# RWKV stage: TensorE in the order of emission, projection banks emptied one step later, weight transfers apart from their casts

## Chip, cores and metric

One core of a Trainium2 chip runs the whole program. The metric is the device time of one execution in microseconds (us); lower is better. TensorE is written PE, VectorE DVE, ScalarE ACT, GpSimd POOL, and the queue that issues most transfers SP.

## The reference

One decoder layer on x (1 x 1024 x 1024, float32): a shared RMSNorm, one input projection, two parallel branches of 16 heads (head size 64), an output projection, a residual and a final RMSNorm. The branch that matters here is the RWKV-7 recurrence:

```
p = rms_norm(x) @ w_in                    # 1024 x 8320
p_tm = p + (shift_by_one(p) - p) * mu     # r, k, v and two low-rank inputs
a = sigmoid(a0 + a_lo @ a_up);  decay = exp(-exp(-softplus(-(w0 + tanh(w_lo) @ w_up)) - 0.5))
state = state * w_t + (state @ -kk_t) (kk_t * a_t) + v_t k_t      # for each of 1024 tokens
y_t = state @ r_t
y = (group_norm(y) + bonus) * silu(gate)
```

The other branch is a dilated sliding-window attention over the same projection. Both go through w_out.

## The kernel before

The RWKV stage works in chunks of 64 tokens. A **unit** is one pair of heads on one half of the sequence (512 tokens, 8 chunks); there are 16 units, and two that follow each other (h = 0, here called even, and h = 1, odd) share a pair of heads. `rwkv` (L284) walks over p = -2 to 15. In each round unit p is in its recurrence (`chain`), unit p+1 in the inversion of its triangular matrices (`late`, `invert`), unit p+2 in its preparation (`prepare`, `products`), and unit p-1 is finished (`finish`). Each of these functions returns steps with the number of one of 24 slots (`NSLOT`); slot by slot the steps are called, and after the steps of a slot `advance(n)` emits n matmuls (4 in the rounds 0 to 12) of the input projection, which runs along through the whole stage as a stream (`stream`, L182).

The recurrence takes three slots per chunk, and each slot is one link of a chain that goes back and forth between three engines:

- slot 3c: `first` multiplies the state Sd into the banks z and T on PE; `spread` copies z to zd, one half on DVE (L704), the other on ACT (L705). [...]
- slot 3c+1: `second` multiplies zd on PE, and `spread` makes ud of it (L707 on DVE, L708 on ACT).
- slot 3c+2: `third` multiplies ud into T on PE, and `spread` makes the next Sd (L707, L708).

All of that is one form of PE matmul on the page (L693: z<-Sd, T<-Vd, T<-Sd, z<-zd, T<-ud, z<-Vd), and the three spreads are what PE waits for. The projection matmuls (L179, 128 x 512, 24 of them for a bank pq) depend on none of it.

Around these lie, in every unit: the products pa of `products` (L559, 16 matmuls on 64 of the rows of PE's array), the small products of the inversion xq, dq, x (L634 and L646 with 32 matmuls of 16 x 16, L663 and L674 with 16 of 32 x 32), transposes through PE, decay and bonus matmuls; on ACT the exponentials W and Ux (L428, L433) of the scans I that DVE makes (L422), the copies Vd (L513), a (L438), the copies Y of the recurrence's output (L745) and its squares ysq (L762); on DVE the inversion's columns TB, UB (L604, L606), the mean gs of Y (L756) and its subtraction (L758).

The projection itself asks two things of the other engines. `wload` (L161) fetches the 256 KB halves of a weight tile (wraw) and splits each into wh (cast on ACT, L170) and wl (subtraction on DVE, L171; on POOL for the attention columns); `stream` calls it for the next job ahead of the first matmul of the current one. `take` empties a full bank pq, for r, k and v by `shift` (ACT L213, then DVE L216).

Which instruction stands where on an engine is not decided by this text alone: a scheduler simulates the program and gives each engine, at each point of its simulated time, the ready instruction that was emitted first. The order that it writes is then fixed, and on the chip each engine executes its own in that order, waiting at its head where an input is late.

Of the kernel before, what the change touches and what calls it, by code (L numbers as in the profile page):

```python
# [33 lines left out]
WARM = (1, 0)  # L34
V_AT = (-2, 3, -1)
# [10 lines left out]
class Kern:  # L46
# [114 lines left out]
    def wload(self, src, wp, eng):  # L161

        nc = self.nc
        wl = wp.tile([128, KT, 128], F32R, name="wl")
        wh = wp.tile([128, KT, 128], F32R, name="wh")
        for i in range(2):
            raw = wp.tile([128, KT // 2, 128], F32, name="wraw")
            ks = slice(4 * i, 4 * i + 4)
            nc.sync.dma_start(out=raw, in_=src[i * 512:(i + 1) * 512].rearrange("(kt p) c -> p kt c", p=128))
            nc.scalar.copy(out=wh[:, ks], in_=raw)  # L170
            eng.tensor_tensor(out=wl[:, ks], in0=raw, in1=wh[:, ks].bitcast(F32), op=ALU.subtract)  # L171
        return wh, wl
# [9 lines left out]
    def stream(self, jobs):  # L182
# [3 lines left out]
        w = load(jobs[0])  # L186
        for i, (_, halves, take) in enumerate(jobs):
            wn = load(jobs[i + 1]) if i + 1 < len(jobs) else None
            for h in halves:
                q = self.ps_proj.tile([128, HALF], F32, name="pq", tag="proj")  # L190
                steps = self.proj_steps(w, h, q)
                for m in steps[:-1]:
                    m()
                    yield
                steps[-1]()
                take(h, q)
                yield
            w = wn
# [85 lines left out]
    def rwkv(self, pairs=range(NPAIR), apairs=range(NPAIR)):  # L284
        nc = self.nc
        with ExitStack() as ctx:
# [40 lines left out]
            N = len(units)  # L327
            self.flow = self.stream(self.jobs(units, apairs))
# [6 lines left out]
            self.lora_w(units[0])  # L335
            for p in range(-2, N):
# [3 lines left out]
                if dC:  # L340
                    put(enumerate(self.chain(dC, get(p + 1) if dC["h"] == 0 else None)))
# [8 lines left out]
                if get(p + 3) and get(p + 3)["h"] == 0:  # L350
                    ev[12].append(lambda d=get(p + 3): self.lora_w(d))
# [18 lines left out]
    def lora_w(self, d):  # L370
# [6 lines left out]
        hi = [self.mid.tile([128, 128], F32R, name=f"lhi{i}", bufs=1) for i in range(2)]  # L377
        lo = self.llo
        for i in range(2):
            a, b = slice(64 * i, 64 * i + 64), slice(64 - 64 * i, 128 - 64 * i)  # L380
            nc.scalar.copy(out=hi[i][a], in_=raw[a])
            nc.scalar.copy(out=hi[i][b], in_=raw[a])
            nc.gpsimd.tensor_tensor(out=lo[i][a], in0=raw[a], in1=hi[i][a].bitcast(F32), op=ALU.subtract)
        d["lw"] = hi, lo

    def prepare(self, d):
# [66 lines left out]
        def norm():  # L453
# [8 lines left out]
            V.reciprocal(out=rn, in_=rn)  # L462
            d["rn1"] = self.mid.tile([64, NC_], F32, name="rn1", bufs=3)
            S.copy(out=d["rn1"], in_=rn[64:128])
# [20 lines left out]
        def bonus_parts():  # L485
            rs = d["rs"]
            V.scalar_tensor_tensor(out=rs, in0=rs, scalar=self.hrk[:, pr:pr + 1], in1=d["ks"], op0=ALU.mult, op1=ALU.mult)
            bh, bl = d["bs"] = [self.tmp(t, n, dt=F32R) for t, n in (("kr3", "bh"), ("vr3", "bl"))]
# [101 lines left out]
    def invert(self, d, U):  # L590
# [86 lines left out]
        def m4c():  # L677
# [4 lines left out]
            (22, m4), (23, m4c)]  # L682
# [481 lines left out]
```

## Time and profile before

| | |
|---|---|
| median of 3 runs | 1554.56 us (1554.13 to 1555.15) |
| the profiled execution | 1555.3 us |
| its span in the profile | 1553.6 us |
| PE busy | 1486.1 us (96%) |
| DVE busy | 1009.3 us (65%) |
| ACT busy | 897.6 us (58%) |
| POOL busy | 442.0 us (28%) |
| granted PE clock, mean of the span | 0.998 |

The profiled execution took 1555.3 us, 1.7 us more than its span and 0.7 us more than the median. PE busy counts from the start of a matmul's record to its modelled end; records overlap, so a busy share near 100% does not say that PE takes a new matmul as often as it could.

### The profile page before, as it was taken

The page shows a single profiled execution, that of the slowest core. Times are in us where ns is not written, and L with a number is a line of the kernel's source. Part 1 is how long each engine was busy: PE and PEld are TensorE (multiplying, and loading weights), DVE is VectorE, ACT ScalarE, POOL GpSimd, SP SyncE. Part 2 cuts the span into 40 slices and gives each one's busy share as a digit, 9 for nine tenths or more (in the row PEclk, how much of TensorE's full clock was granted, in tenths as well). Part 3 has the DMA queues.
Part 4 walks back from the last instruction along what each step waited for, and adds up shares of the span by engine and source line. Part 5 has one row for each costly group of instructions (what it writes and reads, how often), then busy time and mean ns, then how long its engine had stood idle before and what let it go on. Part 6 is the DMA issues. An engine that isn't in the chain of part 4 may idle for free.

```text
span 1553.6 us, 29135 instructions
## 1 busy us (share of the span) xinstructions
PE 1486.1 (96%) x10721; PEld 1201.3 (77%) x10721; DVE 1009.3 (65%) x2776; ACT 897.6 (58%) x2080; POOL 442.0 (28%) x563
## 2 busy tenths in 40 slices
PE   5999999999999999999999999999999999899997
PEld 4877777777777777777777788888888888787886
DVE  6866776667776677766743557667676666956144
ACT  6655666666676666666643556555565565655221
POOL 3211111111111121112211534334443343456442
PEclk9999999999999999999999999999999999999999
DMA  6321111111111111111111201111111111426452
GB/s 199 90 48 33 41 40 39 41 34 40 47 32 41 47 33 41 39 38 41 34 39 34 70 28 42 35 35 34 38 52 34 36 55 55 159 92 203 142 161 99
DMA packets 178829, 94.87 MB, mean 61 GB/s; under 512 B 58413, under 2 KB 164606, under 8 KB 178686
## 3 DMA queue, kind: packets, MB, share of 16 engines
q1 hardware_dynamic: 174942, 86.19, 19.4%
q10 hardware_dynamic: 3744, 6.82, 1.3%
q8 instruction: 84, 1.38, 0.4%
q14 instruction: 59, 0.48, 0.1%
HBM read 75.01 MB, written 17.83 MB: 60 GB/s over the span
## 4 chain that ended last, share of the span: by engine, by line
PE 60%; DVE 17%; ACT 16%; issue 3%; DMA 2%; POOL 1%; SPq 0%; DVEq 0%; ACTq 0%; POOLq 0%
PE pq L179 28%; PE oq L1048 10%; PE o L994 3%; PE z L693 3%; PE T L693 3%; PE mp L921 2%; PE sp L954 2%; ACT Y L745 1%; DVE I L422 1%; ACT MV L569 1%; PE sp L974 1%; ACT Vd L513 1%; DVE TB L604 1%; ACT shtmp L213 1%; PE pa L559 1%
## 5 line engine op out<-in xcount | busy, mean ns | idle before, releaser
L179 PE MATMUL pq<-xh,wh 128*128 128x512 f32 x1040 | 429.1, 413 | 0.0
L179 PE MATMUL pq<-xl,wh 128*128 128x512 f32 x1040 | 412.3, 396 | 0.0
L179 PE MATMUL pq<-xh,wl 128*128 128x512 f32 x1040 | 303.3, 409 | 0.0
L179 PEld LDWEIGHTS pq<-xh,wh 128*128 128x128 f32 x1040 | 195.9, 188 | 32.6 <-ACT xh L157 0.3
L179 PEld LDWEIGHTS pq<-xl,wh 128*128 128x128 f32 x1040 | 196.4, 189 | 30.9 <-DVE xl L158 0.4
L179 PEld LDWEIGHTS pq<-xh,wl 128*128 128x128 f32 x1040 | 184.5, 189 | 31.9
L1048 PE MATMUL oq<-ow,qr 128*128 128x512 f32 x512 | 161.9, 394 | 1.2 <-ACT ow L1029 0.6
L982 POOL TENSOR_TENSOR pl<-p,ph 128x512 fp32r<-128x512 f32 (+2 forms) x96 | 102.3, 1072 | 202.2 <-ACT ph L981 182.4
L923 DVE CUSTOM_DVE_ANT_0 mp<-mp,maskq 128x512 f32<-128x512 f32 (+1 forms) x192 | 105.5, 570 | 68.4 <-PE mp L921 59.9
L977 ACT ACTIVATE p<-p 128x512 f32<-128x512 f32 (+2 forms) x144 | 64.6, 452 | 104.2 <-DVE p L976 103.3
L171 POOL TENSOR_TENSOR wl<-wraw,wh 128x512 fp32r<-128x512 f32 x64 | 85.5, 1354 | 110.4 <-PE pq L179 58.4
L1043 POOL TENSOR_TENSOR vr<-kr,qr 128x512 fp32r<-128x512 f32 (+2 forms) x68 | 90.8, 1340 | 80.5 <-ACT qr L1042 70.0
L1048 PEld LDWEIGHTS oq<-ow,qr 128*128 128x128 f32 x512 | 95.9, 188 | 22.8 <-ACT ow L1029 1.1
L1048 PE MATMUL oq<-ow,vr 128*128 128x512 f32 x256 | 101.2, 395 | 1.9 <-POOL vr L1043 1.9
L170 ACT CAST wh<-wraw 128x512 fp32r<-128x512 f32 x138 | 80.7, 616 | 28.6 <-PE pq L179 23.4
L1042 ACT CAST qr<-kr 128x512 fp32r<-128x512 f32 (+2 forms) x68 | 40.2, 594 | 93.5 <-PE oq L1048 52.0
L976 DVE TENSOR_TENSOR p<-sp,maskt 128x512 f32<-128x512 f32 (+2 forms) x144 | 65.2, 457 | 43.3 <-PE sp L974 41.9
L570 POOL TENSOR_SCALAR_AFFINE_SELECT MV<-MV 64x512 f32<-64x512 f32 x64 | 47.8, 747 | 125.2 <-ACT MV L569 114.2
L708 ACT ACTIVATE ud<-z,rn 64x64 f32<-64x64 f32 x128 | 39.3, 307 | 65.3 <-DVE ud L707 63.6
L707 DVE TENSOR_SCALAR ud<-z,rn 64x64 f32<-64x64 f32 x128 | 34.3, 268 | 58.1 <-PE z L693 57.9
L693 PEld LDWEIGHTS T<-ud,TU 128*128 128x128 f32 x256 | 42.5, 188 | 34.8 <-ACT ud L708 28.2
L708 ACT ACTIVATE Sd<-T,dec 64x64 f32<-64x64 f32 x120 | 36.9, 307 | 53.5 <-DVE Sd L707 52.0
(236 smaller groups left out, 3158.4 us busy)
## 6 DMA issues: line engine op xcount, KB each, us to landing
wraw<-in_w_in_dram SPq DMA_DIRECT2D x138, 256.0 KB
kr<-mixd SPq DMA_DIRECT2D x60, 256.0 KB
oraw<-in_w_out_dram SPq DMA_DIRECT2D x16, 512.0 KB
xt<-in_x_dram SPq DMA_DIRECT2D x8, 512.0 KB
ld<-TU SPq DMA_DIRECT2D x32, 128.0 KB
mixd<-zt SPq DMA_DIRECT2D x16, 256.0 KB
mixd<-gt SPq DMA_DIRECT2D x16, 256.0 KB
xr<-in_x_dram ACTq DMA_DIRECT2D x16, 256.0 KB
```

What stands on the lines that cost most here:

```text
L170: nc.scalar.copy(out=wh[:, ks], in_=raw)
L171: eng.tensor_tensor(out=wl[:, ks], in0=raw, in1=wh[:, ks].bitcast(F32), op=ALU.subtract)
L179: return [lambda i=i, a=a, b=b: self.nc.tensor.matmul(q, lhsT=a, rhs=b, start=(i == 0), stop=(i == len(ops) - 1)) for i, (a, b) in enumera ...
L570: G.affine_select(out=f, in_=f, pattern=[[0, 4], [-1, 2], [1, 64]], compare_op=ALU.is_ge, fill=0.0, base=0, channel_multiplier=-1)
L693: mm = lambda out, w, x, start, stop: nc.tensor.matmul(out, lhsT=w, rhs=f2(x), start=start, stop=stop, skip_group_check=True)
L708: S.activation(out=out[er[1], 1], in_=q[0:64, 64:128], func=AF.Copy, scale=scale[1])
L923: V.tensor_tensor_reduce(out=mp[:, :kn], in0=mp[:, :kn], in1=self.maskq[:, v0:v0 + kn], op0=ALU.add, op1=ALU.max, scale=1.0, scalar=-3e38, ...
L976: V.tensor_tensor(out=p[:, :qn], in0=sp[:, :qn], in1=self.maskt[:, u0:u0 + qn], op=ALU.add)
L977: S.activation(out=p[:, :qn], in_=p[:, :qn], func=AF.Exp)
L982: G.tensor_tensor(out=pl[:, :qn], in0=p[:, :qn], in1=ph[:, :qn].bitcast(F32), op=ALU.subtract)
L1043: nc.gpsimd.tensor_tensor(out=ml, in0=raw, in1=mh.bitcast(F32), op=ALU.subtract)
L1048: nc.tensor.matmul(q, lhsT=m[:, i], rhs=v, start=(k == 0 and j == 0), stop=(k == 15 and j == 2))
```

## The change

- The rounds 0 to 15 are emitted inside `manual_schedule` for PE: there PE's instructions stand in the order in which the program emits them. The other engines are still ordered by the scheduler, and so is PE in the rounds -2 and -1 and after the stage.
- In these rounds a slot is emitted in a new order: the link of the chain, then the takes of the banks filled in the slot before (`pend`), then half of the slot's projection matmuls, then the other steps, then the other half.
- `wload` is cut in three: the transfers at matmul 0 of the current job, the split of the first half at matmul 9, of the second half at matmul 15 (`SPLIT_AT`). This holds for the attention's projection too.
- `lora_w` fetches in slot 6 and casts in slot 12. Some small steps are moved by a slot: rn1 from 5 to 6, `growth` 11 to 12, `decrease` 12 to 13, the three `removal` steps 13 to 15 to 14 to 16, the bonus product 21 to 20 (its cast stays in 21), `m4` 22 to 23.

No instruction is added or removed in kind or size, except that the order decides how often two stand together.

```diff
+SPLIT_AT = (0, 9, 15)
...
-        for i in range(2):
-            raw = wp.tile([128, KT // 2, 128], F32, name="wraw")
+        def fetch():
+            for i in range(2):
+                raws.append(wp.tile([128, KT // 2, 128], F32, name="wraw"))
+                nc.sync.dma_start(out=raws[i], in_=src[i * 512:(i + 1) * 512].rearrange("(kt p) c -> p kt c", p=128))
+
+        def split(i):
...
+        return w, [fetch, lambda: split(0), lambda: split(1)]
...
-                for m in steps[:-1]:
+                for m in steps:
+                    if t in SPLIT_AT and todo:
+                        todo.pop(0)()
+                    t += 1
                     m()
+                    if m is steps[-1]:
+                        if self.pend is None:
+                            take(h, q)
+                        else:
+                            self.pend.append(lambda take=take, h=h, q=q: take(h, q))
                     yield
...
                 for s in range(NSLOT):
+                    chain[s]()
+                    if self.pend is not None:
+                        while self.pend:
+                            self.pend.pop(0)()
+                        self.advance(n // 2)
                     for f in ev[s]:
                         f()
-                    self.advance(n)
+                    self.advance(n if self.pend is None else n - n // 2)
+            for p in (-2, -1):
+                unit(p)
+            self.pend = []
+            with self.tc.manual_schedule(engines={mybir.EngineType.PE}):
+                for p in range(N):
+                    unit(p)
...
-        return [(2, square), (4, squares), (5, norm), (7, decay), (8, rates), (9, logs), (10, lambda: sums(0)), (11, lambda: sums(1)),
-                (11, growth), (12, decrease), (13, removal), (14, removal2), (15, removal3), (16, receptance), (21, bonus_parts)]
+        return [(2, square), (4, squares), (5, norm), (6, norm1), (7, decay), (8, rates), (9, logs), (10, lambda: sums(0)),
+                (11, lambda: sums(1)), (12, growth), (13, decrease), (14, removal), (15, removal2), (16, removal3),
+                (16, receptance), (20, bonus_parts), (21, bonus_split)]
```

Three places in the built order follow. The first is PE in slots 16 and 17 of an even unit: the link z<-zd, the inversion's first product xq (32 matmuls) and the products pa (16 in two groups of 8). Before:

```order
L693 MATMUL z<-zd_127,U_119 66x128
L179 MATMUL pq<-xh_78,wl 128x512
L559 MATMUL pa_5747<-AR_142,BK 128x128
L634 MATMUL xq<-U_118,LT 16x16
L559 MATMUL pa_5748<-AR_142,BK 128x128
L559 MATMUL pa_5747<-AR_142,BK 128x128
L693 MATMUL T_5614<-ud_129,TU 128x128
L693 MATMUL z<-Vd_121,MV 66x128
L634 MATMUL xq<-U_118,LT 16x16 x29
```

Now, the same two slots:

```order
L732 MATMUL z<-zd_127,U_119 66x128
L185 MATMUL pq<-xh_78,wl 128x512 x2
L673 MATMUL xq<-U_118,LT 16x16 x32
L185 MATMUL pq<-xh_78,wl 128x512 x2
L732 MATMUL T_5613<-ud_129,TU 128x128
L732 MATMUL z<-Vd_121,MV 66x128
L185 MATMUL pq<-xh_78,wl 128x512 x2
L598 MATMUL pa_5751<-AR_142,BK 128x128
L598 MATMUL pa_5752<-AR_142,BK 128x128
```

The 32 matmuls of xq stand together now, and a group of pa is no longer cut by others. Counted over the 15 inversions and 14 groups of products that lie between the first and the last link, xq stood in 58 pieces and stands in 15, and pa stood in 56 and stands in 28. All other forms stood in about as many pieces as now.

The second place is ACT around slot 10 of an even unit, between the spreads Sd, zd and ud of its fourth chunk. Before:

```order
L708 ACTIVATE Sd_123<-T_3595,dec 64x64
L428 ACTIVATE W<-I 128x520
L705 COPY zd_127<-z 64x64
L433 ACTIVATE Ux<-I 128x520
L513 COPY Vd_121<-vq 64x4x64 x4
L436 COPY dec<-Ux 64x8
L438 ACTIVATE a<-ta,hk 128x512
L170 CAST wh<-wraw 128x512
L708 ACTIVATE ud_129<-z,rn_2557 64x64
```

Now:

```order
L747 ACTIVATE Sd_123<-T_7105,dec 64x64
L744 COPY zd_127<-z 64x64
L461 ACTIVATE W<-I 128x520
L466 ACTIVATE Ux<-I 128x520
L552 COPY Vd_121<-vq 64x4x64 x4
L469 COPY dec<-Ux 64x8
L471 ACTIVATE a<-ta,hk 128x512
L747 ACTIVATE ud_129<-z,rn_6101 64x64
L176 CAST wh<-wraw 128x512 x2
```

W has moved behind zd and the first cast of the weights behind ud. In odd units W stands ahead of zd, as before, and a has moved behind ud with the cast.

The third place is DVE at the change from an even unit to the odd one, from the last spread Sd of the even unit to the first ud of the odd one (gs is the mean of Y of the unit that has just ended, wl the weights' subtraction). Before:

```order
L707 TENSOR_SCALAR Sd_122<-T_5035,dec 64x64
L171 TENSOR_TENSOR wl<-wraw,wh 128x512
L704 COPY zd_126<-z 64x64
L171 TENSOR_TENSOR wl<-wraw,wh 128x512
L216 SCALAR_TENSOR_TENSOR vs_5341<-pq,om,shtmp 128x512
L756 TENSOR_REDUCE gs<-Y 128x8
L707 TENSOR_SCALAR ud_128<-z,rn 64x64
```

Now:

```order
L746 TENSOR_SCALAR Sd_122<-T_6201,dec 64x64
L795 TENSOR_REDUCE gs<-Y 128x8
L177 TENSOR_TENSOR wl<-wraw,wh 128x512
L743 COPY zd_126<-z 64x64
L230 SCALAR_TENSOR_TENSOR vs_6522<-pq,om,shtmp 128x512
L796 TENSOR_SCALAR gs<-gs 128x8
L177 TENSOR_TENSOR wl<-wraw,wh 128x512
L797 TENSOR_TENSOR Y<-Y,gs 128x512
L746 TENSOR_SCALAR ud_128<-z,rn 64x64
```

The mean gs and the subtraction Y-gs have moved: gs ahead of zd, Y-gs ahead of ud. On ACT the squares ysq, which need Y-gs, now stand ahead of ACT's half of that ud too (before, behind it).

## Rows read from the trace of the kernel before

**Rows 1.** Windows, two stretches of unit 6: length, busy us per engine, clock, DMA.

```profile
413.00:420.00 7.00, 6.16 (x33) 4.59 (x32) 6.22 (x16) 5.72 (x14) 0.71 (x1) 1.00 0.05 12
420.00:430.00 10.00, 10.00 (x120) 7.59 (x119) 5.15 (x13) 3.93 (x13) 1.74 (x4) 1.00 0.26 61
```

**Rows 2.** Timeline of PE: start us, length us, instruction, idle time before it.

```profile
302.36 0.39 PE L179 MATMUL pq<-xl,wh 128*128 128x512 f32 x1
302.58 0.40 PE L179 MATMUL pq<-xh,wh 128*128 128x512 f32 x1
303.14 0.33 PE L693 MATMUL z<-zd,U 128*66 128x128 f32 x1 [0.16 <-ACT zd L705]
```

**Rows 3.** Timeline of PE: first z<-Sd of unit 1 and of unit 13.

```profile
158.10 0.38 PE L693 MATMUL z<-Sd,AR 128*66 128x128 f32 x2
...
726.26 0.38 PE L693 MATMUL z<-Sd,AR 128*66 128x128 f32 x2
```

**Rows 4.** Timeline of PE: xq in pieces, unit 4.

```profile
329.50 0.39 PE L693 MATMUL T<-Vd,MV 128*128 128x128 f32 x2
329.73 0.39 PE L693 MATMUL T<-Sd,AR 128*128 128x128 f32 x2
330.04 0.21 PE L634 MATMUL xq<-U,LT 32*16 32x16 f32 x2
330.18 0.50 PE L179 MATMUL pq<-xh,wl 128*128 128x512 f32 x1
...
332.92 0.64 PE L634 MATMUL xq<-U,LT 32*16 32x16 f32 x58
333.49 0.93 PE L559 MATMUL pa<-AR,BK 64*128 64x128 f32 x10
```

**Rows 5.** Timeline of PE: the link of slot 10, unit 6 (even), unit 7 (odd).

```profile
413.97 0.38 PE L693 MATMUL z<-zd,U 128*66 128x128 f32 x2
...
417.31 0.49 PE L693 MATMUL T<-ud,TU 128*128 128x128 f32 x2 [0.69 <-ACT ud L708]
...
461.09 0.38 PE L693 MATMUL z<-zd,U 128*66 128x128 f32 x2
...
464.67 0.49 PE L693 MATMUL T<-ud,TU 128*128 128x128 f32 x2 [0.47 <-ACT ud L708]
```

**Rows 6.** Timeline of ACT around the same link of unit 6.

```profile
412.44 0.64 ACT L428 ACTIVATE W<-I 128x520 f32<-128x520 f32 x1 [0.61 <-DVE I L422]
...
413.33 0.64 ACT L433 ACTIVATE Ux<-I 128x520 f32<-128x520 f32 x1
413.88 1.48 ACT L513 COPY Vd<-vq 64x256 f32<-64x256 f32 x4
...
415.60 0.81 ACT L438 ACTIVATE a<-ta,hk 128x512 f32<-128x512 f32 x1
...
416.95 0.31 ACT L708 ACTIVATE ud<-z,rn 64x64 f32<-64x64 f32 x1
```

**Rows 7.** Timeline of PE: the link of slot 7, unit 7 (odd).

```profile
454.29 0.43 PE L693 MATMUL z<-zd,U 128*66 128x128 f32 x2
...
457.32 0.49 PE L693 MATMUL T<-ud,TU 128*128 128x128 f32 x2
```

**Rows 8.** Timeline of ACT in that link.

```profile
455.60 0.30 ACT L381 CAST lhi<-lraw 64x128 fp32r<-64x128 f32 x1 [0.59 <-PE zq L400]
```

**Rows 9.** Timeline of PE: the first two links of unit 7 (odd).

```profile
442.33 0.38 PE L693 MATMUL z<-Sd,AR 128*66 128x128 f32 x2
...
445.65 0.49 PE L693 MATMUL T<-ud,TU 128*128 128x128 f32 x2
```

**Rows 10.** Timelines of DVE and ACT around them.

```profile
443.73 0.74 DVE L216 SCALAR_TENSOR_TENSOR vs<-pq,om,shtmp 128x512 f32<-128x512 f32 x1
444.39 0.67 DVE L756 TENSOR_REDUCE gs<-Y 128x8 f32<-128x512 f32 x1
...
446.14 0.63 ACT L762 ACTIVATE ysq<-Y 128x512 f32<-128x512 f32 x1 [0.55 <-DVE Y L758]
```

**Rows 11.** Waits of DVE, 113 to 768 us: us in total, times, longest.

```profile
DVE wl L171 <- PE pq L179: 9.2, 13, 4.0
```

More of the change, by code (lines that the diff above doesn't have):

```diff
@@ L163, in wload @@
         nc = self.nc
-        wl = wp.tile([128, KT, 128], F32R, name="wl")
-        wh = wp.tile([128, KT, 128], F32R, name="wh")
-        for i in range(2):
-            raw = wp.tile([128, KT // 2, 128], F32, name="wraw")
+        w, raws = [], []
+        def fetch():
[3 more added lines that the diff above has]
+        def split(i):
+            if i == 0:
+                w.extend(wp.tile([128, KT, 128], F32R, name=n) for n in ("wh", "wl"))
             ks = slice(4 * i, 4 * i + 4)
[L169 to L172, printed above, removed]
+            nc.scalar.copy(out=w[0][:, ks], in_=raws[i])
+            eng.tensor_tensor(out=w[1][:, ks], in0=raws[i], in1=w[0][:, ks].bitcast(F32), op=ALU.subtract)
+        return w, [fetch, lambda: split(0), lambda: split(1)]
     def proj_steps(self, w, h, q):
@@ L185, in stream @@
                                       self.nc.vector if job[0] < ATT0 else self.nc.gpsimd)
-        w = load(jobs[0])
+        w, steps = load(jobs[0])
+        for f in steps:
+            f()
         for i, (_, halves, take) in enumerate(jobs):
-            wn = load(jobs[i + 1]) if i + 1 < len(jobs) else None
+            wn, todo = load(jobs[i + 1]) if i + 1 < len(jobs) else (None, [])
+            t = 0
             for h in halves:
@@ L327, in rwkv @@
             N = len(units)
+            self.pend = None
             self.flow = self.stream(self.jobs(units, apairs))
@@ L334, in rwkv, with unit @@
             get = lambda n: units[n] if 0 <= n < N else None
-            self.lora_w(units[0])
-            for p in range(-2, N):
+            self.lora_w(units[0])()
+            def unit(p):
                 dA, dI, dC, dF = get(p + 2), get(p + 1), get(p), get(p - 1)
@@ L339, in rwkv @@
                 put = lambda steps: [ev[s].append(f) for s, f in steps]
-                if dC:
-                    put(enumerate(self.chain(dC, get(p + 1) if dC["h"] == 0 else None)))
+                chain = self.chain(dC, get(p + 1) if dC["h"] == 0 else None) if dC else [lambda: None] * NSLOT
                 if dF:
@@ L350, in rwkv @@
                 if get(p + 3) and get(p + 3)["h"] == 0:
-                    ev[12].append(lambda d=get(p + 3): self.lora_w(d))
+                    d = get(p + 3)
+                    ev[6].append(lambda: d.update(split=self.lora_w(d)))
+                    ev[12].append(lambda: d.pop("split")())
                 elif get(p + 3):
@@ L376, in lora_w, with split @@
         nc.sync.dma_start(out=raw[64:128], in_=self.t["a_up"][:, pc])
[L377 to L384, printed above, removed]
+        def split():
+            hi = [self.mid.tile([128, 128], F32R, name=f"lhi{i}", bufs=1) for i in range(2)]
+            lo = self.llo
+            for i in range(2):
+                a, b = slice(64 * i, 64 * i + 64), slice(64 - 64 * i, 128 - 64 * i)
+                nc.scalar.copy(out=hi[i][a], in_=raw[a])
+                nc.scalar.copy(out=hi[i][b], in_=raw[a])
+                nc.gpsimd.tensor_tensor(out=lo[i][a], in0=raw[a], in1=hi[i][a].bitcast(F32), op=ALU.subtract)
+            d["lw"] = hi, lo
+        return split
     def prepare(self, d):
@@ L462, in norm, with norm1 @@
             V.reciprocal(out=rn, in_=rn)
+        def norm1():
             d["rn1"] = self.mid.tile([64, NC_], F32, name="rn1", bufs=3)
-            S.copy(out=d["rn1"], in_=rn[64:128])
+            S.copy(out=d["rn1"], in_=d["rn"][64:128])
         def removal():
```

10 lines of the change are left out of this document (6 added, 4 removed).

## The prediction

> **What bounds the kernel now.** I read the busy time by stretch first. PE is busy nearly everywhere, at a granted clock of 1.00, and yet not evenly so: around slot 10 of unit 6 it is busy 6.16 of 7.0 us while DVE is busy 6.22 and ACT 5.72, and behind them 10.0 of 10 us while DVE falls to about half [rows 1]. So a unit has a part that the chain of spreads sets, with DVE and ACT full, and a part that PE sets.
>
> Then the timeline of PE, by starts and not by lengths. A projection matmul's record lasts 0.39 us, but the next one starts 0.22 us later; records lie over one another, and where the last of them waits, 0.56 us pass between two starts while the profile counts 0.16 us as idle [rows 2]. An idle time below some 0.17 us does not show at all. [...] By busy time (96% in the table) PE has 4% to win; by starts it has more, as follows.
>
> From unit 1 to unit 13 a unit takes (726.26 - 158.10)/12 = 47.35 us [rows 3]. PE's own steps in it: 96 projection matmuls at 0.23 (0.22 to 0.24 between starts) make 22.1; the chain's 48 at 0.22, the distance of two of them [rows 4], 10.6; bonus and decay, six of the projection's shape, 1.4. The 20 transposes have one record where a chain matmul has two, so I take 0.11 each, 2.2. The 64 matmuls of xq and dq take 0.02 each (58 records, two to a matmul, in 0.57 us [rows 4]), 1.3; x has half as many with twice the columns, 1.0; the 16 of pa I estimate at 0.14, between xq's and the chain's, 2.3. Sum 40.9, and to it come the entries into and out of the small forms.
>
> **What a cut costs.** Two records of xq that stand alone start 0.31 us after the pair before them, where 0.22 would be the chain's pace, and the projection matmul behind them starts 0.14 us later, though two records in the long run take 0.02 [rows 4]. So a piece costs about 0.09 + 0.14 - 0.02 = 0.21 us more than the same records inside a run. [...]
>
> Before, a unit has 58/15 + 3 + 56/14 = 10.9 such pieces, 2.3 us; in the new order 4 + 2 = 6, 1.3 us. PE without a wait is therefore 40.9 + 2.3 = 43.2 us before and 42.2 now, and 47.35 - 43.2 = 4.2 us of a unit are waits, nearly all on the chain. The first term of the change is **-1.0 us a unit**. It lies mostly in slots 14 to 19, in the stretch where PE is full, so nothing hides it.
>
> **The chain's waits, place by place.** The second term is what the new order does to those 4.2 us. Since the DVE and ACT work stays the same in kind, I walked through both queues slot by slot with the lengths of the rows, letting each instruction start behind its predecessor and its inputs. Four places carry most of it.
>
> Slot 10, even units. z<-zd to T<-ud takes 3.34 us, in odd units 3.58 [rows 5], where PE's own work needs 1.2 (2.0 before, which had the bonus matmuls here). ACT is the cause: between its halves of zd and ud stand Ux, Vd, dec, a and one weight cast; from a's start to ud 1.35 us pass, a and that cast [rows 6]. In the new order of even units the cast (about 0.6) is behind ud, but W (0.64) is behind zd, and W waits for the last scan, which DVE now does after its half of zd. I estimate that the scan ends about as late as z<-zd starts; then W 0.64, Ux 0.6, Vd 1.5, dec 0.2 (what lies between Vd's end and a), a 0.75, ud 0.31: the link comes to about 4.0, **+0.6**.
>
> Slot 10, odd units. W stays ahead of zd, and a and the cast go behind ud: 3.58 - 1.35 = 2.3, and with DVE's two products of BK and AR ahead of its half of ud 2.65. **-0.9**.
>
> Slots 7 and 8, odd units. The link takes 3.03 us [rows 7] against 2.1 of PE. ACT stood with the cast lhi at the head of its queue, waiting 0.59 us for the decay matmul zq to read the old lhi [rows 8], and ud was behind it. Now the casts stand behind ud: **-1.0** there. Three of them (0.3 each) with th and ta now precede the spread Sd of slot 8: **+0.5**.
>
> Slots 0 and 1, odd units. z<-Sd to T<-ud takes 3.32 us [rows 9]. Now gs, which waits for ACT's two copies of Y, stands ahead of zd, and vs, wl and Y-gs (0.74 [rows 10], the other two about as gs, 0.67) stand ahead of ud on DVE; ACT's half of ud is behind ysq, which needs Y-gs and takes 0.63 [rows 10]. In the walk zd starts about 1.0 us after z<-Sd and lasts 0.2; the three operations behind it end at 3.2, ysq at 3.95, and ACT's half of ud (0.31 [rows 6]) at 4.3: **+1.0**.
>
> These make +0.2 for a pair of units. The remaining slots give a little in even units (slots 0 to 2 and 6, about -0.9 together, where casts and takes no longer stand ahead of the spreads) and cost 0.5 in slot 14, where the cast bh stands ahead of Sd and waits for the bonus product. Over a pair the waits change by about -0.2 to -0.4 us, which is no more than my reading errors; I take -0.2.
>
> **The other edits.** DVE's wl stood 9.2 us, in 13 waits, with PE's projection ahead of it [rows 11], because the split overwrote a buffer still being read. With the splits at matmul 9 and 15 this is over; I have it in the slots above, where a spread stood behind it, and it is nothing elsewhere, since ends of DVE work that no spread waits for are free. The first half of the next weights is needed at matmul 24, 15 matmuls or 3.4 us after its split; cast (0.6, above) and subtraction (as gs, 0.67) need about 1.3. If that cover went, each job would lose what is missing, at most 1.3. In the attention stage jobs have 48 matmuls, so the room is larger; I take 0. The rounds -2 and -1 and the last three units, which do fewer steps, I take as unchanged: the cuts they lose are few and the chain sets their length.
>
> **Sum.** 13 units (0 to 12) by (-1.0 - 0.1) us = -14.3 us. From the profiled execution, 1555.3, that is 1541; it lies 0.7 above the median of the runs shown, so I forecast **1540 us**.
>
> **Rivals.**
> - *The blocked queues count for more.* ACT and DVE no longer stand behind casts and takes that wait for PE; my walk moves each wait only to the next instruction, and an order closer to the machine may let the chain run ahead in slots 2 to 9 too. If a third of the 4.2 us goes: 13 x (1.0 + 1.4) = 31, 1523 us. For it: lhi and wl, each of them a wait with the chain behind it [rows 8, 11]. Against it: in that part DVE is busy 6.22 of 7.0 us [rows 1], and no DVE work goes away.
> - *Slower: ACT's order in slots 9 to 10 and 0 to 1.* Work that itself waits, W for the scan and ysq for Y-gs, stands ahead of ud, and PE, in its fixed order, cannot pass on to anything but two or four projection matmuls. If these two places cost 2.5 and 2.5 us instead of 0.6 and 1.0, a pair loses 3.4 more than it wins 2.4: 6.5 x 1.0 = 7 us slower, 1561 us. It decides from 2.4 us a pair above my sum. [...] The 0.59 us of lhi show such a wait here [rows 8].
> - *Nothing moves.* If the chain sets the whole unit and PE's freed 1.0 us only lengthens its waits, the time stays at 1554. Against it: the 10 us of full PE [rows 1].
>
> **Chances.** Forecast (1533 to 1548) 0.45, blocked queues 0.25, nothing 0.10, slower 0.20. A measurement here tells about 0.2% (3 us) from no change. Faster: 0.45 + 0.25 and a little of the nothing case, 0.72; same 0.10; slower 0.18. The range leaves out a tenth on each side: 1520 to 1559.
>
> **What would show it.** Right: xq in one piece per unit in the timeline and unit starts about 46.2 us apart; slot 10 of about 4.0 us in even units and 2.7 in odd ones; the cast lhi behind ud; slots 0 and 1 of odd units longer by about 1 us. Wrong: unit starts 47 us apart or more with pieces gone, then waits took their place, and the links of slots 0, 1 and 8 to 10 would be the ones to look at; or 45 and less, then the queues that stood behind PE were worth more than the walk says.

## The result, and the profile after

The changed kernel takes 1575.62 us (median of 4 runs, 1575.15 to 1577.04), the kernel before beside it 1554.86 (1554.13 to 1556.13): ratio 1.0138, 95% interval 1.0126 to 1.0150. It is slower by 21 us, where the forecast had 14 us less.

The timeline of PE after the change, first z<-Sd of unit 1 and of unit 13 (columns as in [rows 2]); it answers to [rows 3].

```profile
160.59 0.38 PE L732 MATMUL z<-Sd,AR 128*66 128x128 f32 x2
...
742.07 0.38 PE L732 MATMUL z<-Sd,AR 128*66 128x128 f32 x2
```

A unit now takes (742.07 - 160.59)/12 = 48.46 us instead of 47.35. That is 13.3 us over twelve units; by the same starts unit 0 adds 1.2, units 13 to 15 together 5.8, and the stage begins 1.3 us later. What lies behind the stage gives 1.4 us back (span 1573.8 for 1553.6 us). So the loss is in the stage, and most of it in the units that the prediction summed.

The pieces did go. The timeline of PE in unit 7, where before xq and pa stood in pieces of 2 to 58 records [rows 4]:

```profile
483.44 0.69 PE L673 MATMUL xq<-U,LT 32*16 32x16 f32 x64
485.62 1.16 PE L598 MATMUL pa<-AR,BK 64*128 64x128 f32 x16
```

The windows of the same two stretches of unit 6, slot 10 and what follows, 9 us later in this kernel (they answer to [rows 1]):

```profile
422.00:429.00 7.00, 4.77 (x28) 3.67 (x28) 6.30 (x18) 5.58 (x14) 0.67 (x3) 1.00 0.12 18
429.00:439.00 10.00, 9.73 (x126) 7.48 (x124) 4.66 (x12) 4.61 (x14) 1.37 (x2) 1.00 0.21 56
```

DVE and ACT work as long there as before; PE has fallen from 6.16 to 4.77 of 7 us and stays nearly full behind it, 9.73 of 10 us. PE does less where it had to wait anyway, and hardly less where it is full. The timeline of PE says it in the link of slot 10, unit 6 (even) and unit 7 (odd), against [rows 5]:

```profile
423.18 0.38 PE L732 MATMUL z<-zd,U 128*66 128x128 f32 x2
423.31 1.17 PE L185 MATMUL pq<-xh,wl 128*128 128x512 f32 x4
426.71 0.49 PE L732 MATMUL T<-ud,TU 128*128 128x128 f32 x2 [2.23 <-ACT ud L747]
...
472.37 0.43 PE L732 MATMUL z<-zd,U 128*66 128x128 f32 x2
472.56 1.18 PE L185 MATMUL pq<-xh,wl 128*128 128x512 f32 x4
474.97 0.38 PE L732 MATMUL T<-ud,TU 128*128 128x128 f32 x1 [1.24 <-ACT ud L747]
```

The links last 3.53 and 2.60 us, near the forecast 4.0 and 2.65. But an idle 2.23 us stands in the first, where before 0.69 us did: the fixed order has four projection matmuls here, where the scheduler had put two to three more and the two bonus matmuls. The waits of PE by releaser, 115 to 790 us (us in total, times, longest):

```profile
PE T L732 <- ACT ud L747: 35.0, 31, 2.9
PE z L732 <- ACT Sd L747: 14.3, 27, 1.3
PE z L732 <- ACT zd L744: 7.8, 15, 1.9
```

and the same list of before, 113 to 768 us:

```profile
PE T L693 <- ACT ud L708: 7.6, 14, 0.7
PE z L693 <- ACT zd L705: 4.2, 13, 0.5
PE z L693 <- ACT Sd L708: 3.8, 19, 0.5
```

ACT's order behind the even link, which answers to [rows 6], is as the walk had it (timeline of ACT): zd, W, Ux, four Vd, dec and a stand ahead of ud, the weight casts behind it.

```profile
422.29 0.20 ACT L744 COPY zd<-z 64x64 f32<-64x64 f32 x1 [1.25 <-DVE zd L743]
422.74 0.64 ACT L461 ACTIVATE W<-I 128x520 f32<-128x520 f32 x1 [0.24 <-DVE I L455]
423.28 0.62 ACT L466 ACTIVATE Ux<-I 128x520 f32<-128x520 f32 x1
423.81 1.48 ACT L552 COPY Vd<-vq 64x256 f32<-64x256 f32 x4
425.30 0.20 ACT L469 COPY dec<-Ux 64x8 f32<-64x8 f32 x1
425.52 0.81 ACT L471 ACTIVATE a<-ta,hk 128x512 f32<-128x512 f32 x1
426.36 0.31 ACT L747 ACTIVATE ud<-z,rn 64x64 f32<-64x64 f32 x1
```

A second loss is PE's clock. Windows of the stretch ahead of, in and behind the end of slot 10 in unit 2 (busy us of PE, PEld, DVE, ACT, POOL, then the granted clock):

```profile
227.00:231.00 4.00, 1.77 (x10) 1.11 (x8) 3.75 (x10) 3.87 (x10) 0.67 (x3) 1.00 0.09 20
231.00:234.00 3.00, 3.00 (x9) 2.61 (x10) 1.24 (x4) 1.42 (x3) 0.00 (x0) 0.50 0.18 17
234.00:238.00 4.00, 4.00 (x24) 3.20 (x24) 3.61 (x8) 1.20 (x3) 0.10 (x1) 0.95 0.23 62
```

Behind the wait of slot 10 the granted clock was 0.50 for 3 us, and 0.95 in the mean of the 4 us that follow. It was 0.50 as well behind slot 10 of units 4 (330.0 to 333.0 us) and 8 (524.6 to 527.6 us). The periods of units 2, 4 and 8 are 49.5 us against 47.9 to 48.2 in the even units 6, 10 and 12: 1.2 to 1.6 us each, some 4 us in all. Below, such a stretch at a granted clock of 0.50 is called a fall of the clock. Before, every window of 2 us from 100 to 800 us, units 1 to 12 among them, shows 1.00.

### The profile page after: what moved, and what is told of

It is laid out like the page before. It is cut to its first block, busy times and chain, and to the rows that moved or that the text cites. A ratio compares the mean times of both kernels' runs of the same rounds, so it can differ in the third digit from the quotient of the medians.

```text
span 1573.8 us, 29071 instructions
## 1 busy us (share of the span) xinstructions
PE 1470.0 (93%) x10721; PEld 1183.1 (75%) x10721; DVE 1024.8 (65%) x2776; ACT 895.2 (57%) x2080; POOL 434.4 (28%) x563
## 4 chain that ended last, share of the span: by engine, by line
PE 62%; DVE 19%; ACT 14%; issue 3%; DMA 2%; POOL 0%; DVEq 0%; SPq 0%; ACTq 0%; POOLq 0%
PE pq L185 29%; PE oq L1087 10%; PE T L732 4%; PE o L1033 3%; PE z L732 3%; PE mp L960 2%; PE sp L993 2%; PE pa L598 2%; DVE TB L643 2%; ACT Vd L552 1%; DVE UB L645 1%; DVE I L455 1%; DVE TU L605 1%; PE sp L1013 1%; ACT zt L825 1%
## 5 line engine op out<-in xcount | busy, mean ns | idle before, releaser
L185 PE MATMUL pq<-xh,wh 128*128 128x512 f32 x1040 | 440.9, 424 | 0.0
L185 PE MATMUL pq<-xh,wl 128*128 128x512 f32 x1040 | 314.5, 413 | 0.0
L185 PEld LDWEIGHTS pq<-xh,wl 128*128 128x128 f32 x1040 | 179.7, 190 | 26.6
L732 PE MATMUL T<-ud,TU 128*128 128x128 f32 x256 | 56.0, 300 | 40.4 <-ACT ud L747 39.3
L746 DVE TENSOR_SCALAR Sd<-T,dec 64x64 f32<-64x64 f32 x120 | 32.8, 273 | 54.4 <-PE T L732 53.7
```

The costliest lines, as they stand in the source:

```text
L185: return [lambda i=i, a=a, b=b: self.nc.tensor.matmul(q, lhsT=a, rhs=b, start=(i == 0), stop=(i == len(ops) - 1)) for i, (a, b) in enumera ...
L732: mm = lambda out, w, x, start, stop: nc.tensor.matmul(out, lhsT=w, rhs=f2(x), start=start, stop=stop, skip_group_check=True)
L746: V.tensor_scalar(out=out[er[0], 0], in0=q[0:64, 0:64], scalar1=scale[0], scalar2=None, op0=ALU.mult)
```

## Where the links went

For every slot I took the length of its link, from the first matmul of one link to that of the next in the timeline of PE, and the number of projection matmuls that stand in it in PE's order. The table has them summed over neighbouring slots: means of even units 6, 10, 12 (no fall of the clock among them) and of odd units 3, 5, 9, 11; us, and the matmuls behind the bar. Runs e1, e2 and e15 are told below.

```
even     before    after     e2        e1        e15
0-2      6.33|14   5.56|12   6.39|12   5.56|12   6.25|12
3-5      4.56|10   5.11|12   4.98|12   5.02|12   5.46|12
6        2.25|4    2.06|4    2.45|4    2.04|4    2.00|4
7-9      5.65|12   5.99|12   5.63|12   6.00|12   5.17|7
10       3.34|6    3.54|4    2.67|4    3.58|7    2.57|10
11-13    5.13|16   4.67|12   5.08|12   4.92|14   4.93|11
14-19   12.40|18  12.97|24  12.52|24  11.69|19  12.94|24
20-21    4.18|8    4.40|8    3.94|8    3.94|8    3.93|8
22-23    3.34|8    3.68|8    3.34|8    3.68|8    3.34|8
unit    47.18     47.99     47.00     46.42     46.59
odd
0-2      5.20|12   6.23|12   5.21|12   5.66|12   5.28|12
3-5      5.18|12   4.99|12   5.43|12   5.41|12   5.40|12
6        1.66|4    2.30|4    1.96|4    2.03|4    1.96|4
7-9      6.80|12   6.32|12   6.05|12   6.23|12   5.80|7
10       3.57|7    2.57|4    3.15|4    3.57|7    2.57|10
11-13    4.76|13   4.68|12   5.23|12   5.02|14   5.05|11
14-19   12.88|20  12.47|24  12.52|24  11.45|19  12.95|24
20-21    4.16|8    4.85|8    3.94|8    4.39|8    3.94|8
22-23    3.33|8    3.68|8    3.33|8    3.68|8    3.34|8
unit    47.55     48.09     46.83     47.44     46.28
```

## The experiments

Each starts from the changed kernel, from the one before or from an earlier run, as its edit says, and was timed in rounds against the kernel before on the same chip (medians there 1553.4 to 1554.7 us).

**Which part costs: PE's fixed order, or the rest?** Theory A put the loss on DVE's and ACT's work ahead of the spreads, which the other edits bring; theory B on the fixed order. Run e1 is the changed kernel with the scheduler ordering PE again; run e2 is the kernel before with nothing but PE in the order of emission.

```diff
 e1, against the changed kernel          e2, against the kernel before
-with self.tc.manual_schedule(...PE):   +with self.tc.manual_schedule(...PE):
-    for p in range(N):                 +    for p in range(N):
-        unit(p)                        +        unit(p)
+for p in range(N):
+    unit(p)
```

> The changed kernel with PE ordered by the scheduler again, all other edits kept. Theory A (the chain waits longer because DVE and ACT work that waits itself, or that is long, now stands ahead of the spreads in slots 1, 6, 10 and 20; that order comes from the other edits): still slow, 1567 to 1578 us, the link of slot 10 in even units still about 3.5 us. Rival B (the fixed order of PE is what costs, since PE may no longer take projection matmuls forward while the chain is late): back to 1555 or below.

Measured: 1551.96 us, ratio 0.9988 (0.9978 to 0.9997). Theory A falls: with all other edits in place and only PE given back to the scheduler, the loss is gone.

> The kernel before with the fixed PE order in the rounds 0 to 15 and nothing else: all steps of a slot, then its four projection matmuls; takes and weight splits where they were. Theory A: the pieces of xq and pa go (1.0 us a unit) and the waits stay near 4.7 us a unit, 1538 to 1550 us. Rival B: 1565 us or more.

Measured: 1556.69 us, ratio 1.0017 (1.0007 to 1.0027). Theory B falls too: the fixed order by itself costs 2 us. The 21 us are neither part's but come of both together. The table says how. In e1 the links of even units are nearly those of the changed kernel (slot 10 3.58 for 3.54, slots 22 and 23 3.68 in both; in odd units slot 10 grows from 2.57 to 3.57), but PE is less idle in them. The timeline of PE in e1, slot 10 of unit 6:

```profile
413.93 0.38 PE L731 MATMUL z<-zd,U 128*66 128x128 f32 x2
414.07 1.65 PE L185 MATMUL pq<-xh,wl 128*128 128x512 f32 x6
416.13 0.50 PE L571 MATMUL bq<-bh,bdr 128*128 128x512 f32 x1 [0.42 <-ACT Vd L551]
416.47 0.39 PE L571 MATMUL bq<-bl,bdr 128*128 128x512 f32 x1
416.70 0.40 PE L185 MATMUL pq<-xh,wl 128*128 128x512 f32 x1
417.52 0.38 PE L731 MATMUL T<-ud,TU 128*128 128x128 f32 x1 [0.42 <-ACT ud L746]
```

Seven projection matmuls and the bonus stand in a link of the same length, and slots 14 to 19, where PE is full, are left with 19 of them in place of 24: 11.7 and 11.5 us instead of 13.0 and 12.5. In e2 every slot has its four as well, but there the sum of the links is shorter, by 1.0 and 1.3 us a unit: 2.67 us in slot 10 of even units, 3.94 us in slots 20 and 21, 3.34 in 22 and 23 (odd slot 10 is longer, 3.15). The profiled execution of e2 even gains on the kernel before where the prediction had its sum: 46.89 us a unit from unit 1 to 13 instead of 47.35. It loses 2.3 us in unit 0. One caution: when PE's order is fixed, the scheduler writes other orders for DVE and ACT too. In the traces, some 330 of DVE's 2776 instructions and 67 of ACT's 2080 stand elsewhere in e1 (buffer numbers left out), so e1 undoes more than PE's order.

**The later splits and takes.** Run e3 makes fetch and both splits of the next weights at matmul 0 of a job; run e4 empties a bank in the slot in which it fills.

```diff
 e3                                     e4
-SPLIT_AT = (0, 9, 15)                  -if self.pend is None:
+SPLIT_AT = (0,)                        -    take(h, q)
-    if t in SPLIT_AT and todo:         -else:
+    while t in SPLIT_AT and todo:      -    self.pend.append(lambda ...: take(h, q))
                                        +take(h, q)
```

> The changed kernel with the weight transfers and both splits at matmul 0 of the current job, as before. Theory A has the splits at 9 and 15 as one of the moves that put wl and wh between the spreads of slots 0, 1 and 22, 23: 3 to 8 us faster than the changed kernel if they matter, 1568 to 1572. Rival B: as the changed kernel, 1574 to 1577; or slower, if casts that wait for PE's last reading of the old weights cost more.

Measured: 1581.97 us, ratio 1.0177 (1.0162 to 1.0193).

> The changed kernel with each bank emptied in the slot that fills it, as before. Theory A: the takes (about 1.4 us of ACT and DVE, every sixth slot) come ahead of the spreads again; waits in slots 0, 6, 12 and 18 grow, 1576 to 1585 us, or fall by as much if the later take is what now stands ahead of ud: 1568. Rival B: no change, 1574 to 1577.

Measured: 1581.80 us, ratio 1.0177 (1.0160 to 1.0194). In the changed kernel each of these two edits is worth 6 us, so they are not what costs. Part of the 6 us can be clock: between the first and the last unit the traces of e3 and e4 show four and six falls, that of the changed kernel three (granted clock from 720 to 900 us 0.98 and 0.97, against 1.00). Nor are the 6 us a property of the fixed order alone: e12 below keeps both edits and takes as long as e2, which has neither.

**Is the idle time of the long links room for PE?** Theory C: DVE and ACT set a long link's length, and the fixed four matmuls leave it unfilled. Rival D: the casts and takes make the chain longer, and filling is no use. Run e7 deals the 96 projection matmuls of a unit unevenly in the changed kernel, run e8 in e2.

```diff
+FILL = ({10: 8, 15: -2, 16: -2, 17: -2, 19: -2},                         # e7, even units
+        {1: 4, 2: -2, 10: 5, 15: -2, 16: -2, 17: -2, 19: -1})             # e7, odd units
+FILL = ({10: 6, 15: -2, 16: -2, 17: -2}, {10: 8, 15: -2, 16: -2, 17: -2, 19: -2})   # e8
...
+n = base + (FILL[p % 2].get(s, 0) if p >= 0 and base == 4 else 0)
```

> The changed kernel, with projection matmuls dealt out unevenly: in slot 10 there are 12 of them (even units) or 9 (odd), in slot 1 of odd units 8, taken from slots 2 and 15 to 19, 96 a unit as before. Theory C (unfilled links): the links z<-zd to T<-ud of slot 10 and of odd slot 1 last what ACT and DVE need (3.54, 2.59 and 2.29 us), whatever PE does meanwhile, and a fixed four matmuls cover 1.1 us of them, where the scheduler put six or seven. Then the links keep their lengths within 0.3 us, about 2.0 us a unit goes from slots 15 to 19, 13 x 2.0 = 26 us, and the time is 1543 to 1553. Rival D (the new places of casts and takes make the chain itself longer): what is dealt to slot 10 comes on top of the link or goes to the wait behind it, 1565 to 1582.

Measured: 1562.80 us, ratio 1.0051 (1.0036 to 1.0066): 13 us of the expected 26, between the two theories' ranges, and in units 1 to 12 no fall of the clock is left (granted clock from 115 to 720 us 1.00, in the changed kernel 0.99), which alone is worth some 4. PE's wait in even slot 10 fell from 2.41 to 0.19 us (link less PE's own work, at the paces of the prediction), but slot 13 got one of 0.95.

> The kernel before with TensorE in the order of emission, and with the same uneven dealing: 10 (even units) or 12 (odd) projection matmuls in slot 10, taken from slots 15 to 19. Theory C: slot 10's waits of 1.54 and 1.95 us in that kernel are covered, 1.4 and 1.8 us a unit less, 13 x 1.6 = 21 us below 1556.7: 1533 to 1542, faster than both kernels. Rival D: 1550 to 1565.

Measured: 1555.99 us, ratio 1.0010 (1.0000 to 1.0020), no gain over e2 and inside rival D's range. The waits of slot 10 fell from 1.54 and 1.95 us to 0.82 and 0.02, and in slot 11 the links grew from 1.94 to 3.01 and 3.27 us. In this dealing a bank fills in slot 10 and not in slot 11, and its take and the next split come with it; so it does not separate C from D.

**The order inside a slot, and the slots of the small steps.** Run e9 emits all four matmuls behind the slot's other steps; run e5 puts norm, growth, decrease, removal, bonus and the last product of the column solve back into their old slots.

```diff
-        self.advance(n // 2)
     for f in ev[s]:
         f()
-    self.advance(n if self.pend is None else n - n // 2)
+    self.advance(n)
```

That was e9; e5 changes numbers in the lists of slots:

```diff
-(5, norm), (6, norm1), (12, growth), (13, decrease), (14, removal), (15, removal2), (16, removal3), (20, bonus_parts), (23, m4)
+(5, lambda: (norm(), norm1())), (11, growth), (12, decrease), (13, removal), (14, removal2), (15, removal3), (21, bonus_parts), (22, m4)
```

> The changed kernel with all four projection matmuls of a slot behind the slot's other steps, instead of two ahead and two behind. Theory C: every link still holds four, so the time stays at 1571 to 1580. Rival F (the two ahead of the steps are what delays transposes and the chain's supply): 1565 or less.

Measured: 1569.19 us, ratio 1.0095 (1.0080 to 1.0110). C's claim for it fails, and F's 1565 is not reached: the number of matmuls in a link stayed, but links changed. Slots 20 and 21 got shorter (4.40 and 4.85 us to 3.93), and slot 1 of odd units (2.29 to 1.59); slots 22 and 23 grew by 0.34 us, slot 10 of odd units by 0.65.

> The changed kernel with the small steps (norm, growth, decrease, the three of removal, the bonus split, the last product of the column solve) back in the slots that they had before. Theory C: they lie outside the long links, so 1568 to 1580. Rival G (these moves put work ahead of the spreads, and are the loss): 1562 or less.

Measured: 1565.66 us, ratio 1.0072 (1.0057 to 1.0087), below what C allowed and above rival G's 1562. Slots 22 and 23 went from 3.68 back to 3.33 us in both kinds of unit, 0.35 x 13 = 4.5 us of the 10; units 13 to 15 together give 4.0. In slot 10 even units have 2.62 us for 3.54, odd ones 3.65 for 2.57: the two have changed places, and the timeline of ACT in e5, even unit 6, shows why:

```profile
421.68 0.64 ACT L461 ACTIVATE W<-I 128x520 f32<-128x520 f32 x1 [1.40 <-DVE I L455]
422.34 0.20 ACT L744 COPY zd<-z 64x64 f32<-64x64 f32 x1
422.57 0.64 ACT L466 ACTIVATE Ux<-I 128x520 f32<-128x520 f32 x1
423.12 1.49 ACT L552 COPY Vd<-vq 64x256 f32<-64x256 f32 x4
424.63 0.20 ACT L469 COPY dec<-Ux 64x8 f32<-64x8 f32 x1
424.86 0.31 ACT L747 ACTIVATE ud<-z,rn 64x64 f32<-64x64 f32 x1
425.19 0.82 ACT L471 ACTIVATE a<-ta,hk 128x512 f32<-128x512 f32 x1
```

W stands ahead of zd and a behind ud, so ud starts 2.26 us after z<-zd (which starts at 422.60) and not 3.18 us as in the changed kernel. Same steps, another order from the scheduler.

**Both cures, and the small steps without the fixed order.** Run e12 is e5 and e9 together, run e11 is e1 and e5 together.

> The changed kernel with both partial cures: small steps back in their old slots (-10 us alone) and the four projection matmuls behind a slot's other steps (-6.4 alone). If the places of the losses are separate (slots 22, 23 and 10 there, 1 and 20 here), the sum holds: 1556 to 1562. If each cure only made the scheduler deal ACT's and DVE's steps differently, it does not: 1563 to 1572.

Measured: 1556.55 us, ratio 1.0010 (1.0001 to 1.0020). The sum holds (1575.6 - 10.0 - 6.4 = 1559.2), and the three falls of the clock in units 1 to 12, which e5 and e9 each still have, are gone here too (granted clock from 115 to 720 us 0.99 in e5 and in e9, 1.00 here): under the fixed order the moved small steps and the two matmuls ahead account for 19 of the 21 us.

> TensorE by the scheduler again and the small steps back in their old slots: of the change only the later takes, the transfers and casts apart, and the projection matmuls in two halves are left. Theory C: with the slot moves undone slots 22 and 23 give back 0.35 us a unit (they did with the fixed order, 3.34 for 3.69 us), 1544 to 1550, faster than both kernels. Rival: the scheduler makes the slot moves count for nothing, and the time stays within 2 us of 1552.

Measured: 1549.54 us, ratio 0.9972 (0.9961 to 0.9982), faster than both kernels. The same edit that is worth 10 us under the fixed order is worth 2.4 us where the scheduler orders PE. Its expectation asked for more than 2 us and got that; the gain of 0.35 us in slots 22 and 23 is there, but the scheduler had hidden the other losses.

**ACT in the order of emission.** Theory H: the scheduler runs ACT's W, Ux, dec and a, written for slots 12 and 13, ahead of slot 10's ud; in the order of emission the link must shrink. Rival I: the work only moves. In run e14 PE and ACT stand in the order of emission, in e13 DVE too.

```diff
-manual_schedule(engines={PE})
+manual_schedule(engines={PE, Activation})          # e14; in e13 {PE, Activation, DVE}
```

> The changed kernel with PE and ACT in the order of emission, DVE by the scheduler. Theory H: as above for ACT's half, 1540 to 1565. Rival I: 1568 to 1600.

Measured: 1614.36 us, ratio 1.0389 (1.0374 to 1.0405).

> The changed kernel with ACT and DVE in the order of emission too, as PE. Theory H: slot 10's link is long because W, Ux, dec and a, written in slots 12 and 13, and the Vd copies were put ahead of the spread ud by the scheduler, which runs ACT ahead; in the order of emission they stand behind the spreads of slots 10 to 13, slot 10's link falls from 3.54 us to 2.0 or less in even units, and the waits of a unit by 1 to 3 us: 1535 to 1562. Rival I (ACT and DVE are full in slots 8 to 14 and their work only moves, or later steps now wait for it): slot 10 shorter, other links longer by as much, 1565 to 1600.

Measured: 1673.55 us, ratio 1.0761 (1.0735 to 1.0787). H is right on the link and wrong on the time. The timeline of PE in e14, slot 10 and, 12 us ahead of it, slot 5 of unit 6:

```profile
428.31 0.49 PE L732 MATMUL T<-ud,TU 128*128 128x128 f32 x2
...
431.31 0.66 PE L817 MATMUL yq<-ident,Y 128*128 128x128 f32 x4 [1.83 <-DVE Y L811]
431.72 0.71 PE L185 MATMUL pq<-xh,wl 128*128 128x512 f32 x2
432.27 0.38 PE L732 MATMUL z<-Sd,AR 128*66 128x128 f32 x2
...
440.53 0.38 PE L732 MATMUL z<-zd,U 128*66 128x128 f32 x2
440.67 1.18 PE L185 MATMUL pq<-xh,wl 128*128 128x512 f32 x4
441.68 0.43 PE L732 MATMUL T<-ud,TU 128*128 128x128 f32 x2
```

Slot 10 is down from 3.54 to 1.15 us: what stood ahead of ud on ACT did make that link. But slot 5 takes 3.96 us for 1.83, since PE in its fixed order stops at the transpose of Y and the chain's z<-Sd stands behind it, though its own input had been there for 2.8 us; ACT's half of Sd ended at 429.46 (timeline of ACT):

```profile
429.15 0.31 ACT L747 ACTIVATE Sd<-T,dec 64x64 f32<-64x64 f32 x1 [0.89 <-DVE Sd L746]
```

Both runs are slower than rival I allowed, too. In the changed kernel, where the scheduler orders ACT, PE waited for DVE's Y ahead of the 64 transposes once, 1.7 us in all; in e14 the wait above alone is 1.83 us. So I take it that ACT's work that runs ahead feeds such steps in time.

**Filling within a bank.** Runs e15 and e16 fill slot 10 from slots 7, 9 and 11 of the same bank, so that no take or split moves; e15 in e12, e16 in the changed kernel. Run e6 undoes the last untested part, the small up weights' fetch and cast in two slots.

```diff
+FILL = {7: -2, 9: -3, 10: 6, 11: -1}               # e15 and e16
...
-ev[6].append(lambda: d.update(split=self.lora_w(d)))   # e6
-ev[12].append(lambda: d.pop("split")())
+ev[12].append(lambda: self.lora_w(d)())
```

> The kernel with both partial cures, with ten projection matmuls in slot 10 instead of four, taken from slots 7, 9 and 11 just around it, so that every projection bank still ends in the slot where it did. Theory C (PE's own work in slots 7, 9 and 11 sets their links, and slot 10's wait of 1.64 and 1.93 us is room for six matmuls): slot 10 keeps 2.8 and 3.1 us, slots 7, 9 and 11 lose 0.46, 0.69 and 0.23, 13 x 1.38 = 18 us less, 1536 to 1544. Rival I (DVE and ACT are full from slot 7 to slot 13, and the stretch lasts what their queues need): slot 10 grows by what slots 7 and 9 lose, 1553 to 1560.

Measured: 1547.18 us, ratio 0.9953 (0.9936 to 0.9969).

> The changed kernel with the same dealing of projection matmuls. Theory C: slot 10's waits are 2.41 and 1.45 us; 13 x 1.38 = 18 us less, and the three falls of the clock go too: 1553 to 1558. Rival I: 1570 to 1577.

Measured: 1565.64 us, ratio 1.0072 (1.0057 to 1.0087).

> The changed kernel with the small up weights fetched and cast in one step of slot 12 again, as before. By the prediction's step on the casts lhi (they stood at the head of ACT's queue in odd slot 7, 1.0 us) odd slot 7 grows again and the time is 1577 to 1583; if the scheduler's order matters more than the step's slot, it stays within 1572 to 1577.

Measured: 1576.02 us, ratio 1.0137 (1.0122 to 1.0152); the fetch's own slot does nothing. Filling gave 9.4 us of 18 in e15. In e16 it gave 10 of 22, since there C also counted the three falls of the clock, which are gone from units 1 to 12 (granted clock from 115 to 720 us 1.00); the links alone give 0.6 us a unit in both runs. Both times lie between the two theories' ranges, and both theories hold by half: the timeline of PE in e15, slot 10 of unit 6, has no wait at its end,

```profile
411.57 0.43 PE L732 MATMUL z<-zd,U 128*66 128x128 f32 x2 [0.65 <-ACT zd L744]
...
412.99 1.29 PE L186 MATMUL pq<-xh,wl 128*128 128x512 f32 x5
414.12 0.27 PE L732 MATMUL T<-ud,TU 128*128 128x128 f32 x1
```

but an idle 0.65 us now stands ahead of it, in slot 9, which gave matmuls up, and slot 11 grew by 0.2 to 0.3 us. So over slots 7 to 13 DVE and ACT seem to keep part of the length, however PE is dealt; only this dealing was tried.

**More of the same.** Run e17 is e15 with `14: 2, 16: -2` added and, in even units, `{0: -2, 1: 4, 2: -2}`.

> The dealing that won (ten projection matmuls in slot 10), and two more long links filled from slots beside them within the same bank: slot 1 of even units (waits 1.18 us) gets eight, from slots 0 and 2; slot 14 (0.50 us) gets six, two of them from slot 16. Theory C: 6.5 x 0.9 and 13 x 0.45 us less than 1547.2, 1533 to 1540. Rival I (the queues of DVE and ACT set the length of these stretches as well): the waits go to the slots beside them, half of the gain or less, 1541 to 1549.

Measured: 1542.25 us, ratio 0.9928 (0.9911 to 0.9944): 4.9 us of the 12 that C promised, inside rival I's range. It is the fastest version of this study, 11 us ahead of the kernel before on the same chip and 33 ahead of the changed one.

## Why the prediction was wrong

The forecast's change by place, in its own steps, and the measured one (after less before in the table):

```
place             even: forecast  measured    odd: forecast  measured
0-2 and 6                -0.9       -0.96
0-2                                                +1.0       +1.03
3-5                       0         +0.55           0         -0.19
6                                                   0         +0.64
7-9                       0         +0.34          -0.5       -0.48
10                       +0.6       +0.20          -0.9       -1.00
11-13                     0         -0.46           0         -0.08
14-19                    -0.5       +0.57          -1.0       -0.41
20-21                     0         +0.22           0         +0.69
22-23                     0         +0.34           0         +0.35
unit                     -0.8       +0.81          -1.4       +0.54
```

- **The step that failed** is the first term, "-1.0 us a unit": "It lies mostly in slots 14 to 19, in the stretch where PE is full, so nothing hides it". The pieces went as counted: a unit has 6 instead of 11 (xq 1 for 4, pa 2 for 4), 1.05 us at the prediction's 0.21. What the term left out is that the new order also moves projection matmuls. Before, the scheduler had 18 or 20 of them in slots 14 to 19 and more than four a slot in slots 10 to 13 (in even units in 0 to 2 too); the fixed order brings the stretch back to 24. Four to six matmuls at 0.23 are 0.9 to 1.4 us, as much as the pieces had cost, and the stretch went from 12.40 and 12.88 us to 12.97 and 12.47, on average no gain. PE's work fell in slot 10 instead, by 0.9 and 1.1 us, where it waits for ud in any case. The other runs agree: with 24 matmuls the stretch takes 12.5 (e2) or 12.9 us (e15), with 19, and xq still in 2.5 pieces, 11.7 and 11.5 (e1). This step is 0.83 us of the 1.78 us a unit between forecast and result.
- **The bookkeeping behind it.** The walk added changes of link lengths to a change of PE's total. Closer is a sum over the links of the longer of chain and PE: work that PE loses in a link that the chain sets is worth nothing, and work that comes back to one that PE sets costs in full. That is a first estimate and not a law shown here: the runs that filled waits gave half of what it promises, or nothing (e8).
- **Places that the walk took as zero**: 22-23 (+0.35 in all units; the inversion's last product, moved from 22 to 23, and e5 gives it back), 20-21 (+0.22 and +0.69; UT and both TU stand ahead of Sd on DVE there, and e9 gives it back), odd slot 6 (+0.64), even slots 3-5 and 7-9. Slots 20 to 23 alone are 0.80 us of the 1.78. The timelines of DVE and ACT in slot 20 of unit 7 show the second of them; ACT's copies MV wait for TU, its half of Sd stands behind them, and PE waits for that half until 494.79:

```profile
491.80 0.71 DVE L694 STREAM_TRANSPOSE UT<-U 128x512 f32<-128x512 f32 x1 [1.42 <-ACT U L691]
492.43 1.36 DVE L605 TENSOR_TENSOR TU<-pa,mask 64x512 f32<-64x512 f32 x2
493.82 0.28 DVE L746 TENSOR_SCALAR Sd<-T,dec 64x64 f32<-64x64 f32 x1
...
493.11 1.30 ACT L608 COPY MV<-pa 64x512 f32<-64x512 f32 x2 [1.01 <-DVE TU L605]
494.43 0.31 ACT L747 ACTIVATE Sd<-T,dec 64x64 f32<-64x64 f32 x1
```

- **What held**: slot 10 in odd units (-1.00 for -0.9), slots 0 to 2 in both, slots 7 to 9 in odd units (the casts lhi stand behind ud and slot 7 takes 2.12 us for 3.03; it takes as long in e6, where fetch and casts are in one step again, so it was not the edit of `lora_w` that moved them). Slot 10 in even units had the right mechanism and came out 0.4 us better.
- **The "other edits" and the last three units**: late splits and takes were put at zero and save 6 us each in the changed kernel (e3, e4), and nothing together where the small steps and the matmuls stand as before (e12 against e2). Units 13 to 15, taken as unchanged, lost 5.8 us; e1 and e17 have some of that back (39.5 and 41.3 us for unit 14, against 43.7 after and 40.0 before). I did not look for its cause.
- **The clock**, some 4 us, was in no term.

Averaged over the two kinds of unit the measured change is +0.68 us where -1.1 was forecast, 1.78 x 13 = 23 us; with the last units and the clock it is 33 of the 36 us between forecast and result; the later start of the stage and the shorter rest behind it cancel. Of the rivals the slower one had the right sign and half of the mechanism: PE "cannot pass on to anything but two or four projection matmuls". The places that it named, slots 9 and 10 and 0 and 1, are not where the loss is.

By edits and not by places, the runs say it more firmly: the fixed order alone costs 2 us (e2), the other edits alone nothing (e1), the moved small steps under the fixed order 10 (e5) and the two matmuls ahead of a slot's steps 6.4 (e9), both together 19 (e12).

What stays open: why the scheduler puts W and a ahead of zd and ud in one kind of unit and behind them in the other. A run with DVE's and ACT's orders held word for word and only PE's changed was not made, so how much of e1's gain is PE's own order, and how much the other engines' new ones, is shown only by place in the table.

## What to carry to other kernels

Before fixing an engine's order by hand, count what the scheduler had put into each long wait: the cover of a wait is part of the tuned state, and a uniform dealing takes it away. Price a change link by link, first as the longer of chain and engine, and not as total work plus total waits. Try a fixed order and moved steps apart: here neither cost more than some 2 us without the other, and both together cost 21. A dealing by hand can beat the scheduler when the fill comes from slots beside the wait and moves no other step; here it gave back half of the idle time that it filled, or a little less.

## What the hardware showed

PE's granted clock fell to 0.50 behind idle stretches of slot 10 in three even units of the changed kernel (2, 4 and 8), and not in units 6, 10 and 12 (1.00), although that link lasts 3.53 to 3.55 us and idles 2.22 to 2.24 us in all six. Each fall cost 1.2 to 1.6 us. Of units 1 to 12, three had one in e5 (odd links of 3.65 us) and in e9 (3.22 us), two in e3 (even links of 3.15 us). In e1, where the link lasts 3.6 us and PE idles 0.85 us in it, none had one; nor in e12, with links of 2.8 and 3.1 us that idle 1.5 and 1.8 us. The granted clock, as a mean from 115 to 720 us, was 0.99 in the changed kernel, e5 and e9, and 1.00 in e1, e12 and, with its two falls, e3. So the same link can bring a fall in one unit and none in the next, and the runs do not say what decides.
